# Softmax heads and stick-breaking heads in a pipeline of pairs, in a two-layer decoder trunk on one core

## The chip, the cores and the metric

The kernel runs on one core of a Trainium2 chip. The metric is the device time of one execution in microseconds. The median of three runs of the kernel before is 1323.23 us.

## The reference

Two layers, each with two gated feed-forward blocks around a mixer and a cross attention. The change touches the mixer alone:

```python
SEQ, D_MODEL, HEAD_DIM = 256, 1024, 64
N_FOX, N_DSA, N_SB = 6, 5, 5

def hybrid_mixer(h, positions, w_in, b_fgate, w_fox_out, w_dsa_out, w_sb_out, w_out):
    proj = h @ w_in
    ...
    # FOX: softmax(q k^T * scale + c_q - c_k, causal) v, c = cumsum of log forget gates
    o_fox = fox_attention(fq, fk, fv, log_f).reshape(b, s, FOX_W)
    # DSA: softmax over the top 64 keys of an index score
    o_dsa = dsa_sparse_attention(dq, dk, dv, q_idx, k_idx, w_idx, topk).reshape(b, s, DSA_W)
    # stick-breaking: a = exp(log_sigmoid(z) + sum of log_sigmoid(-z) over the keys between)
    o_sb = stick_breaking_attention(sq, sk, sv).reshape(b, s, SB_W)
    g = jax.nn.sigmoid(gates.reshape(b, s, N_BRANCH, D_MODEL))
    merged = g[:, :, 0] * (o_fox @ w_fox_out) + g[:, :, 1] * (o_dsa @ w_dsa_out) + g[:, :, 2] * (o_sb @ w_sb_out)
    return merged @ w_out
```

## The kernel before

Activations lie with features on the partitions (`xT`, eight tiles of 128 x 256). Every projection is three fp32r matmuls per 128 x 128 weight tile (`mm3`, L139 to L141): weight high by activation high, high by low, low by high. `load_w` brings a weight tile by DMA (SyncE's queue, `wraw`, three buffers), casts the high part on ScalarE (L92, `wh`, five buffers) and subtracts the low part on VectorE or sometimes GpSimd (L86, `wl`, five buffers). Matmuls of attention are plain fp32.

The mixer of a layer is written in this order: index heads and their top-k mask; FOX (three pairs of heads, L665 to L688); DSA (two pairs and a head, from L691); gate projections 0 to 4 (`gate_proj`) and the first sigmoids; stick-breaking (two pairs and a head, L780 to L815); `merge(0)`; the transposes of the memory (`transposed`, L243) with its squares and their statistics (`stats`, L197 and L199; `newton` with Ln and Exp makes the scale `rm` from them); gate projections 5 to 11; `sigmoids(4, 12)`; `merge(1)`; the keys of the cross attention from the memory; `merge(2)`; the split of the merged branches; `w_out`.

The code only gives dependencies. The order on each engine is made by a list scheduler that works through a simulated timeline, so projections of later parts are drawn in between attention steps. `tc.issue_after(x)` puts what follows behind x, if both are on the same engine. PSUM has three banks `acc` for projections, two `qk` for scores, two `tr` for transposes and statistics, one `ops` for products with v.

A softmax pair runs so: scores of two heads (L671 adds the key decay through a mask matmul, L675 is q times k with 64 rows for each head, on the two halves of the rows), logits into `w384` on VectorE, maximum, Exp on ScalarE, scaling by the reciprocal sum; `softmax_pv` then transposes (L606), copies to SBUF on ScalarE and multiplies with v (L618, L619). A stick-breaking pair has scores (L792), Abs, Exp and Ln on ScalarE, a split into high and low part, a running sum by matmuls with a triangular matrix `negu` into the `qk` banks (L804 to L808), two additions and an Exp, and the product with v.

`table(name)` loads a set of ScalarE's function tables. It stands behind all activations collected in `tabs["ops"]` since the last load, and each `tact` stands behind the load:

```python
def table(name):
    with ExitStack() as es:
        for i in tabs["ops"]:
            es.enter_context(tc.issue_after(i.ins))
        tabs["load"] = ACT.preload_act_table_set(name)
    tabs["ops"] = []
```

`sigmoids(c0, c1)` loads the table of the sigmoid, does the gates c0 to c1 and loads the table of Ln and Exp again. In `merge(br)` four accumulators `acc` are filled in turn, and VectorE multiplies each with its gate (L737), which frees the bank.

Of the kernel before, what the change touches and what calls it, by code (L numbers as in the profile page):

```python
# [9 lines left out]
F32 = mybir.dt.float32  # L10
# [3 lines left out]
OP = mybir.AluOpType  # L14
# [18 lines left out]
def trunk(ctx: ExitStack, tc: tile.TileContext, x, mem, positions, ffn1_norm, ffn1_w_gu, ffn1_w_down,  # L33
# [426 lines left out]
    def mixer_cross(l):  # L460
# [4 lines left out]
        with tc.tile_pool(name="mix", bufs=1) as mp:  # L465
# [122 lines left out]
            def softmax_pv(lgs, v, h0, ot):  # L588


                for p in lgs:
                    nm = mp.tile([128, 2], F32, name="nm", bufs=4)
                    sm = mp.tile([128, 2], F32, name="sm", bufs=4)
                    for t, (c0, c1) in enumerate((Q0, Q1)):
                        DVE.tensor_reduce(nm[:, t:t + 1], p[:, c0:c1], axis=AX.X, op=OP.max, negate=True)
                        tact(p[:, c0:c1], p[:, c0:c1], AF.Exp, bias=nm[:, t:t + 1], accum_out=sm[:, t:t + 1])
                    rs = mp.tile([128, 2], F32, name="rsm", bufs=4)
                    DVE.reciprocal(rs, sm)
                    for t, (c0, c1) in enumerate((Q0, Q1)):
                        last = DVE.tensor_scalar(p[:, c0:c1], p[:, c0:c1], rs[:, t:t + 1], None, op0=OP.mult)  # L600
                pTs = []
                for p in lgs:
# [4 lines left out]
                    pT = w384()  # L607
                    last_copy = ACT.activation(pT, ps[:, :384], AF.Copy)
                    pTs.append(pT)
                with tc.issue_after(last_copy.ins):  # L610
                    for i, pT in enumerate(pTs):
                        pv(ot, v, h0 + i, pT[:, 0:256], pT[:, 256:384])
# [53 lines left out]
            ofox = []  # L666
            for j in range(NFOX // 2):
# [9 lines left out]
                ot = o_ps()  # L677
                lgs = []
                for i, ps in enumerate(bank):
                    h = 2 * j + i  # L680
                    lg = w384()
                    DVE.scalar_tensor_tensor(lg[:, 0:128], ps[:, 0:128], cq[:, 0, h:h + 1], cmask[:, 0:128],
                                             op0=OP.add, op1=OP.add)
                    DVE.scalar_tensor_tensor(lg[:, 128:384], ps[:, 256:512], cq[:, 1, h:h + 1], cmask[:, 128:384],
                                             op0=OP.add, op1=OP.add)
                    lgs.append(lg)
                softmax_pv(lgs, fv, 2 * j, ot)
                ofox.append(hsplit(ot, 2))  # L688
# [11 lines left out]
            odsa = []  # L700
            for j in range(3):
                nh = 2 if j < 2 else 1
                bank = scores(dT[0][j], dT[1][j], nh)
                ot = o_ps()
                lgs = []
                for i, ps in enumerate(bank):
                    lg = w384()
                    DVE.tensor_tensor(lg, ps[:, :384], dmask, op=OP.add)
                    lgs.append(lg)
                softmax_pv(lgs, dv, 2 * j, ot)  # L710
                odsa.append(hsplit(ot, nh))
# [68 lines left out]
            for j in range(3):  # L780
                nh = 2 if j < 2 else 1

                zm = mp.tile([128, 2, 384], F32, name="zm", bufs=1)
                az = mp.tile([128, 2, 384], F32, name="az", bufs=1)
                sph = mp.tile([128, 2, 384], F32R, name="sph", bufs=1)
                spl = mp.tile([128, 2, 384], F32R, name="spl", bufs=1)
                zm, az, sph, spl = zm[:, :nh], az[:, :nh], sph[:, :nh], spl[:, :nh]
                bank = [qk_ps() for _ in range(nh)]
                for c, q0, k0 in ((0, 0, 0), (256, 128, 128)):
                    for i, ps in enumerate(bank):  # L790
                        b = slice(64 * i, 64 * i + 64)
                        PE.matmul(ps[:, c:c + 256 - q0], sk[j][b, k0:k0 + 128], sq[j][b, q0:], start=True, stop=True)  # L792
                for i, ps in enumerate(bank):
                    DVE.tensor_tensor(zm[:, i], ps[:, :384], smask, op=OP.add)
                ACT.activation(az, zm, AF.Abs)
                tact(az, az, AF.Exp, scale=-1.0)
                tact(az, az, AF.Ln, bias=1.0)
                DVE.scalar_tensor_tensor(az, zm, 0.0, az, op0=OP.max, op1=OP.add)
                split(sph, spl, az)
                ps0, ps1 = qk_ps(), qk_ps()  # L800
                p0 = ps0[:, :nh * 256].rearrange("p (h n) -> p h n", h=nh)
                p1 = ps1[:, :nh * 256].rearrange("p (h n) -> p h n", h=nh)
                for v in (sph, spl):
                    PE.matmul(p0, negu, v[:, :, 0:256], start=v is sph, stop=False)  # L804
# [154 lines left out]
```

## Time and profile before

| | us |
|---|---|
| median of three runs | 1323.23 (1323.03 to 1323.39) |
| profiled execution, whole time | 1323.02 |
| its span in the trace | 1321.3 |
| TensorE busy | 1305.2 |
| VectorE busy | 894.0 |
| ScalarE busy | 746.3 |
| GpSimd busy | 295.8 |

The profiled execution is one more run, within 0.2 us of the median; its span leaves out 1.7 us around the work. The mixer of layer 1 lies at about 198 to 445 us of the span, that of layer 2 at about 850 to 1093 us. In a timeline row the first number is the start, the second how long the group of equal instructions took. Matmuls overlap in the pipeline, so the pace is the distance of starts, not the length in the row.

### The profile page before, as it was taken

The page shows a single profiled execution, that of the slowest core. Times are in us where ns is not written, and L with a number is a line of the kernel's source. Part 1 is how long each engine was busy: PE and PEld are TensorE (multiplying, and loading weights), DVE is VectorE, ACT ScalarE, POOL GpSimd, SP SyncE. Part 2 cuts the span into 40 slices and gives each one's busy share as a digit, 9 for nine tenths or more (in the row PEclk, how much of TensorE's full clock was granted, in tenths as well). Part 3 has the DMA queues.
Part 4 walks back from the last instruction along what each step waited for, and adds up shares of the span by engine and source line. Part 5 has one row for each costly group of instructions (what it writes and reads, how often), then busy time and mean ns, then how long its engine had stood idle before and what let it go on. Part 6 is the DMA issues. An engine that isn't in the chain of part 4 may idle for free.

```text
span 1321.3 us, 26329 instructions
## 1 busy us (share of the span) xinstructions
PE 1305.2 (99%) x10746; PEld 1273.2 (96%) x10746; DVE 894.0 (68%) x1389; ACT 746.3 (56%) x1191; POOL 295.8 (22%) x267
## 2 busy tenths in 40 slices
PE   8999999999999999999999999999999999999997
PEld 7999998999999999999999999998999999999987
DVE  6866656966769776665666665569767686866644
ACT  6555544466775575554465554444667755655543
POOL 3211024322314121111121110243224230311100
PEclk9999999999999999999999999999999999999999
DMA  8555655544646555666655565645355655566551
GB/s 256 192 191 186 221 162 154 174 142 124 187 133 218 163 179 172 197 196 202 194 190 192 192 204 180 197 137 177 103 166 165 199 192 161 178 195 196 196 181 62
DMA packets 220712, 234.65 MB, mean 178 GB/s; under 512 B 8656, under 2 KB 209968, under 8 KB 220592
## 3 DMA queue, kind: packets, MB, share of 16 engines
q1 hardware_dynamic: 219904, 231.87, 55.1%
q8 instruction: 84, 1.38, 0.5%
q0 software_dynamic: 240, 0.55, 0.1%
q10 hardware_dynamic: 448, 0.57, 0.1%
q14 instruction: 36, 0.29, 0.1%
HBM read 231.91 MB, written 1.05 MB: 176 GB/s over the span
## 4 chain that ended last, share of the span: by engine, by line
PE 94%; DVE 2%; DMA 1%; issue 1%; POOL 1%; ACT 1%; DVEq 0%; ACTq 0%; POOLq 0%
PE acc L139 29%; PE acc L141 28%; PE acc L140 28%; DVE wl L86 1%; PE qk L553 1%; PE ops L618 1%; PE qk L675 1%; DMA wraw<-in_ffn_w_gu_dram 1%; DVE t L154 1%; PE ops L619 1%; PE tr L606 0%; POOL it L527 0%; DMA wraw<-in_w_in_dram 0%; PE qk L861 0%; PE qk L792 0%
## 5 line engine op out<-in xcount | busy, mean ns | idle before, releaser
L86 DVE TENSOR_TENSOR wl<-wraw,wh 128x1024 fp32r<-128x1024 f32 (+4 forms) x427 | 512.7, 1204 | 224.2 <-ACT wh L92 210.9
L92 ACT ACTIVATE wh<-wraw 128x1024 fp32r<-128x1024 f32 (+4 forms) x471 | 465.5, 994 | 245.1 <-PE acc L140 156.6
L141 PE MATMUL acc<-xh,wl 128*128 128x256 f32 x2032 | 563.5, 278 | 0.9 <-DVE wl L86 0.9
L139 PE MATMUL acc<-xh,wh 128*128 128x256 f32 x2032 | 563.9, 279 | 0.0
L140 PE MATMUL acc<-xl,wh 128*128 128x256 f32 x2032 | 563.7, 278 | 0.0
L139 PEld LDWEIGHTS acc<-xh,wh 128*128 128x128 f32 x2032 | 381.2, 188 | 3.8 <-issue 3.3
L141 PEld LDWEIGHTS acc<-xh,wl 128*128 128x128 f32 x2032 | 381.8, 188 | 2.4 <-DVE wl L86 1.7
L140 PEld LDWEIGHTS acc<-xl,wh 128*128 128x128 f32 x2032 | 382.2, 188 | 0.8 <-issue 0.7
L383 POOL TENSOR_TENSOR hm<-sg,gu 128x256 f32<-128x256 f32 x88 | 85.0, 966 | 385.2 <-ACT sg L69 385.2
L141 PE MATMUL acc<-hh,wl 128*128 128x256 f32 x528 | 145.3, 276 | 0.0
L140 PE MATMUL acc<-hl,wh 128*128 128x256 f32 x528 | 145.3, 276 | 0.0
L139 PE MATMUL acc<-hh,wh 128*128 128x256 f32 x528 | 144.3, 276 | 0.0
L86 POOL TENSOR_TENSOR wl<-wraw,wh 128x1024 fp32r<-128x1024 f32 (+4 forms) x44 | 89.9, 2043 | 211.9 <-ACT wh L92 174.1
L69 ACT ACTIVATE sg<-gu 128x256 f32<-128x256 f32 x88 | 36.7, 417 | 120.4 <-DVE gu L379 120.4
L141 PEld LDWEIGHTS acc<-hh,wl 128*128 128x128 f32 x528 | 99.1, 188 | 0.0
L140 PEld LDWEIGHTS acc<-hl,wh 128*128 128x128 f32 x528 | 99.1, 188 | 0.0
L139 PEld LDWEIGHTS acc<-hh,wh 128*128 128x128 f32 x528 | 98.5, 188 | 0.0
L379 DVE TENSOR_TENSOR gu<-acc,rs_r 128x512 f32<-128x512 f32 x88 | 60.3, 686 | 42.3 <-PE acc L141 42.2
L230 POOL TENSOR_TENSOR sqa<-sqa,sq 128x256 f32<-128x256 f32 x54 | 51.9, 960 | 138.8 <-ACT sq L225 137.2
L153 ACT ACTIVATE hh<-hm 128x256 fp32r<-128x256 f32 x88 | 36.1, 410 | 54.0 <-POOL hm L383 54.0
L154 DVE TENSOR_TENSOR hl<-hm,hh 128x256 fp32r<-128x256 f32 x88 | 37.0, 421 | 42.5 <-ACT hh L153 42.4
L141 PE MATMUL acc<-wh,xl 128*128 128x320 f32 (+1 forms) x192 | 61.0, 318 | 0.0
(283 smaller groups left out, 1971.3 us busy)
## 6 DMA issues: line engine op xcount, KB each, us to landing
wraw<-in_ffn_w_gu_dram SPq DMA_DIRECT2D x87, 1024.0 KB, 5.3
wraw<-in_w_in_dram SPq DMA_DIRECT2D x34, 1024.0 KB, 5.4
wraw<-in_ffn_w_down_dram SPq DMA_DIRECT2D x28, 896.0 KB, 4.9
wraw<-in_ffn_w_down_dram SPq DMA_DIRECT2D x18, 1024.0 KB, 5.2
wraw<-in_w_in_dram SPq DMA_DIRECT2D x20, 640.0 KB, 4.1
wraw<-in_ca_w_kv_dram SPq DMA_DIRECT2D x8, 1024.0 KB, 5.0
wraw<-in_w_out_dram SPq DMA_DIRECT2D x8, 1024.0 KB, 5.0
wraw<-in_ca_w_q_dram SPq DMA_DIRECT2D x4, 1024.0 KB, 5.3
```

The costliest lines, as they stand in the source:

```text
L69: i = ACT.activation(*a, **k)
L86: share["last"] = eng.tensor_tensor(lo, raw, h.bitcast(F32), op=OP.subtract)
L92: ACT.activation(h, raw, AF.Copy)
L139: PE.matmul(ps, a[0], b[0], start=first, stop=False)
L140: PE.matmul(ps, a[0], b[1], start=False, stop=False)
L141: PE.matmul(ps, a[1], b[0], start=False, stop=last)
L153: ACT.activation(h, src, AF.Copy)
L154: DVE.tensor_tensor(lo, src, h.bitcast(F32), op=OP.subtract)
L230: POOL.tensor_tensor(n, sqacc[0], sq, op=OP.add)
L379: DVE.tensor_tensor(gu, ps.rearrange("p (i n) -> p i n", i=2), rb2(r), op=OP.mult)
L383: POOL.tensor_tensor(hm, sg, gu[:, 1], op=OP.mult)
L553: PE.matmul(ps[:, c:c + n], q[b, qs], k[b, 0:n], start=True, stop=True)
```

## The change

Softmax heads: `softmax_pv`, which did one pair to its end, is replaced by `attention(npairs, v, score, logits)`, which runs over `npairs + 2` steps. In step n TensorE has one stretch: the transposes of pair n-1, the product with v of pair n-2, the scores of pair n. The stretch stands behind the last scaling of pair n-1 by means of `issue_after` on its first transpose. Then come the copies of the transposes, the logits and the softmax of pair n. FOX and DSA hand over their own functions for scores and logits.

Stick-breaking heads: the loop over three pairs becomes five steps of the same kind. A step holds the running sum of pair n-1, the product with v of pair n-2 and the scores of pair n. The running sum goes into the two `tr` banks, no longer `qk`, with the low part first; the last Exp is one for each head and goes into `w384`.

```diff
-            def softmax_pv(lgs, v, h0, ot):
...
-                pTs = []
-                for p in lgs:
-                    ps = tr_ps()
-                    with tc.issue_after(last.ins):
-                        for j in range(3):
-                            PE.transpose(ps[:, j * 128:(j + 1) * 128], p[:, j * 128:(j + 1) * 128], ident)
...
+            def attention(npairs, v, score, logits):
+                prs, pTs, out, last = {}, {}, [], None
+                for n in range(npairs + 2):
+                    bank, tps, ot = [], [], None
+                    with ExitStack() as es:
+                        if last is not None:
+                            es.enter_context(tc.issue_after(last.ins))
+                        for p in prs.pop(n - 1, ())[::-1]:
+                            ps = tr_ps()
+                            for j in (2, 1, 0):
+                                i = PE.transpose(ps[:, j * 128:(j + 1) * 128], p[:, j * 128:(j + 1) * 128], ident)
+                                if not tps and j == 2:
+                                    es.enter_context(tc.issue_after(i.ins))
+                            tps.insert(0, ps)
+                        if n - 2 in pTs:
+                            ot = o_ps()
+                            for i, pT in enumerate(pTs[n - 2]):
+                                pv(ot, v, 2 * n - 4 + i, pT[:, 0:256], pT[:, 256:384])
+                        if n < npairs:
+                            bank = score(n)
+                    if tps:
+                        pTs[n - 1] = []
+                        for ps in tps:
+                            pT = w384()
+                            last = ACT.activation(pT, ps[:, :384], AF.Copy)
+                            pTs[n - 1].append(pT)
+                    lgs = [logits(n, i, ps) for i, ps in enumerate(bank)]
+                    if ot is not None:
+                        out.append(hsplit(ot, len(pTs.pop(n - 2))))
...
+                            last = DVE.tensor_scalar(p[:, c0:c1], p[:, c0:c1], rs[:, t:t + 1], None, op0=OP.mult)
+                    prs[n] = lgs
+                return out
...
-            for j in range(3):
...
-                ps0, ps1 = qk_ps(), qk_ps()
...
+            for n in range(3 + 2):
...
+                    if 0 <= n - 1 < 3:
...
+                        ps0, ps1 = tr_ps(), tr_ps()
...
+                        for v in (spl, sph):
+                            i = PE.matmul(p0, negu, v[:, :, 0:256], start=v is spl, stop=False)
+                            if v is spl:
+                                es.enter_context(tc.issue_after(i.ins))
...
+                    if 0 <= n - 2:
+                        ot = o_ps()
+                        for i, p in enumerate(prs[n - 2]):
+                            pv(ot, sv, 2 * n - 4 + i, p[:, 0:256], p[:, 256:384])
+                    if n < 3:
+                        bank = [qk_ps() for _ in range(nh)]
...
+                    prs[n - 1] = [w384() for _ in range(mh)]
+                    for i, p in enumerate(prs[n - 1]):
+                        tact(p, mz[:, i], AF.Exp)
+                    last = tabs["ops"][-1]
```

What the scheduler makes of it, at three places of layer 1. Line numbers of the later parts of the mixer are larger by 12 or more in the changed kernel (L671 and L675 are L689 and L693, L606 is L601, L737 is L749).

TensorE at the scores of FOX pair 2. `qk_3169` and `qk_3170` are the banks of its two heads, `acc` rows are projections. Before:

```order
L140 MATMUL acc_3498<-wl_3484,xh2_84 128x320
L671 MATMUL qk_3169<-cneg_80,sel_79 128x256 x2
L675 MATMUL qk_3169<-t1_3009,t1_2885 128x128
L675 MATMUL qk_3169<-t1_3009,t1_2885 128x256
L141 MATMUL acc_3498<-wh_3483,xl2_92 128x320
L671 MATMUL qk_3170<-cneg_80,sel_79 128x256 x2
L675 MATMUL qk_3170<-t1_3009,t1_2885 128x128
L675 MATMUL qk_3170<-t1_3009,t1_2885 128x256
L139 MATMUL acc_3497<-wh_3483,xh3_85 128x320
```

After:

```order
L139 MATMUL acc_3699<-xh5_87,wh_3695 128x256
L601 MATMUL tr_3146<-ident_73,w384_3123 128x128 x3
L601 MATMUL tr_3150<-ident_73,w384_3120 128x128 x3
L689 MATMUL qk_3154<-cneg_80,sel_79 128x256 x2
L689 MATMUL qk_3155<-cneg_80,sel_79 128x256 x2
L693 MATMUL qk_3154<-t1_3009,t1_2885 128x128
L693 MATMUL qk_3155<-t1_3009,t1_2885 128x128
L693 MATMUL qk_3154<-t1_3009,t1_2885 128x256
L693 MATMUL qk_3155<-t1_3009,t1_2885 128x256
L140 MATMUL acc_3699<-xl5_95,wh_3695 128x256
```

The two heads' scores were apart with a projection between; now they are one piece, behind the six transposes of pair 1.

TensorE at the statistics of the memory (L197). `acc_4749` and `acc_4810` are gate projections; `acc_5013`, `acc_5032`, `acc_5064`, `acc_5083` are the four accumulators of merge(1). Before:

```order
L141 MATMUL acc_4749<-xh7_89,wl_4746 128x256
L197 MATMUL tr_4542<-sqa_4540,triones_74 128x256 [waits Pool_49]
L199 MATMUL tr_4542<-triones_74,sqa_4540 128x1 x2
L139 MATMUL acc_4810<-xh0_82,wh_4802 128x256
L140 MATMUL acc_4810<-xl0_90,wh_4802 128x256
```

After:

```order
L145 MATMUL acc_5032<-osp_3683,wl_5009 128x256
L146 MATMUL acc_5032<-osp_3684,wl_5009 128x256
L197 MATMUL tr_4549<-sqa_4547,triones_74 128x256 [waits Pool_49]
L199 MATMUL tr_4549<-triones_74,sqa_4547 128x1 x2
L139 MATMUL acc_5064<-osp_3647,wh_5055 128x256 [waits DVE_49,Activation_49]
...
L146 MATMUL acc_5064<-osp_3684,wl_5060 128x256
L139 MATMUL acc_5083<-osp_3647,wh_5055 128x256 [waits DVE_49,PE_49]
```

The statistics moved from between two gate projections to behind the second accumulator of merge(1). `acc_5083` begins with a wait for VectorE.

ScalarE at Ln and Exp of these statistics (`rs_a`, `rs_b`) and the sigmoids of gates 4 to 11 (`t2`). Before:

```order
L69 ACTIVATE rs_a_4547<-rs_m_4546 128x258 [waits DVE_49]
L153 ACTIVATE sph_4320<-az_4319 128x384 [waits DVE_49]
L69 ACTIVATE rs_b_4548<-rs_a_4547 128x258 [waits Activation_49]
L92 ACTIVATE wh_4928<-wraw_4922 128x1024 [waits PE_49]
L92 ACTIVATE wh_4997<-wraw_4993 128x1024 [waits DMAHW2_49,PE_49,Pool_49]
L69 ACTIVATE az_4319<-zm_4318 128x384 [waits DVE_49,Activation_49]
L64 ACT_TABLE_LOAD
L69 ACTIVATE t2_3992<-t2_3992 128x512
L69 ACTIVATE t2_4615<-t2_4615 128x512
```

After:

```order
L92 ACTIVATE wh_5167<-wraw_5163 128x1024 [waits DMAHW1_49,PE_49]
L92 ACTIVATE wh_5171<-wraw_5163 64x512 [waits DMAHW3_49,PE_49]
L69 ACTIVATE rs_a_4554<-rs_m_4553 128x258 [waits DVE_49]
L69 ACTIVATE rs_b_4555<-rs_a_4554 128x258 [waits Activation_49]
L64 ACT_TABLE_LOAD
L69 ACTIVATE t2_3992<-t2_3992 128x512
L69 ACTIVATE t2_4622<-t2_4622 128x512
...
L64 ACT_TABLE_LOAD
L92 ACTIVATE wh_5218<-wraw_5214 128x1024 [waits DMAHW4_49,PE_49]
```

The table load now follows `rs_b` directly, and `rs_a` ahead of it waits for `rs_m` on VectorE. Six more sigmoids are left out before the last load shown. VectorE around `rs_m` and the product with gate 4, `acc_5006` before and `acc_5013` after. Before:

```order
L86 TENSOR_TENSOR wl_5049<-wraw_5044,wh_5048 128x1024 [waits DMAHW5_49,Activation_49]
L86 TENSOR_TENSOR wl_5053<-wraw_5044,wh_5052 64x512 [waits PE_49,DMAHW7_49,Activation_49,Pool_49]
L719 TENSOR_TENSOR t2_4981<-acc_4932,rs_r_2511 128x512 [waits PE_49]
L86 TENSOR_TENSOR wl_5098<-wraw_5095,wh_5097 128x1024 [waits DMAHW0_49,DVE_49,Activation_49]
L737 TENSOR_TENSOR t2_3992<-acc_5006,t2_3992 128x512 [waits PE_49]
L86 TENSOR_TENSOR wl_5102<-wraw_5095,wh_5101 128x1024 [waits PE_49,Activation_49]
```

After:

```order
L86 TENSOR_TENSOR wl_5109<-wraw_5102,wh_5108 128x1024 [waits PE_49,Activation_49]
L86 TENSOR_TENSOR wl_5168<-wraw_5163,wh_5167 128x1024 [waits DVE_49,DMAHW1_49,PE_49,Activation_49]
L187 TENSOR_SCALAR rs_m_4553<-tr_4549 128x258 [waits PE_49]
L190 TENSOR_TENSOR rs_a_4554<-rs_b_4555 128x258 [waits Activation_49]
L191 SCALAR_TENSOR_TENSOR rs_a_4554<-rs_a_4554,rs_m_4553 128x258 [waits DVE_49]
L192 SCALAR_TENSOR_TENSOR rs_r_4556<-rs_a_4554,rs_b_4555 128x258 [waits DVE_49]
L749 TENSOR_TENSOR t2_3992<-acc_5013,t2_3992 128x512 [waits Activation_49]
```

Two weight splits (`wl_5109`, `wl_5168`, both with a wait for TensorE), `rs_m` and the rest of the statistics now stand ahead of the product with gate 4, and that product waits for ScalarE.

## Rows read from the trace of the kernel before

**Rows 1.** The page: busy time of the engines, granted clock, chain that ended last.

```profile
PE 1305.2 (99%) x10746; PEld 1273.2 (96%) x10746; DVE 894.0 (68%) x1389; ACT 746.3 (56%) x1191; POOL 295.8 (22%) x267
...
PEclk9999999999999999999999999999999999999999
...
PE 94%; DVE 2%; DMA 1%; issue 1%; POOL 1%; ACT 1%; DVEq 0%; ACTq 0%; POOLq 0%
```

**Rows 2.** Waits of TensorE: for what, total us, times, longest.

```profile
PE tr L270 <- DMA xin<-in_x_dram: 5.0, 1, 5.0
```

**Rows 3.** Busy time by window, FOX of layer 2: length, PE, PEld, DVE, ACT, POOL.

```profile
905.00:915.00 10.00, 10.00 (x65) 9.07 (x64) 9.59 (x29) 5.90 (x13) 3.09 (x4) 1.00 0.46 142
```

**Rows 4.** TensorE's timeline, FOX pairs 1 and 2 of layer 1: start, us, instruction.

```profile
256.14 0.64 PE L671 MATMUL qk<-cneg,sel 128*128 128x256 f32 x4
256.70 0.93 PE L675 MATMUL qk<-t,t 64*128 64x128 f32 x8
257.56 0.42 PE L139 MATMUL acc<-wh,xh 128*128 128x320 f32 x1
257.81 0.31 PE L140 MATMUL acc<-wl,xh 128*128 128x320 f32 x1
257.96 0.31 PE L141 MATMUL acc<-wh,xl 128*128 128x320 f32 x1
...
261.04 0.40 PE L671 MATMUL qk<-cneg,sel 128*128 128x256 f32 x2
...
262.47 0.39 PE L671 MATMUL qk<-cneg,sel 128*128 128x256 f32 x2
...
263.90 0.31 PE L140 MATMUL acc<-wl,xh 128*128 128x320 f32 x1
```

**Rows 5.** TensorE's timeline, memory statistics of layer 1 and projections behind.

```profile
373.66 0.59 PE L197 MATMUL tr<-sqa,triones 128*128 128x256 f32 x2
...
374.66 0.28 PE L140 MATMUL acc<-xl,wh 128*128 128x256 f32 x1
...
376.94 0.28 PE L139 MATMUL acc<-xh,wh 128*128 128x256 f32 x1
```

**Rows 6.** TensorE's timeline, FOX pair 3 of layers 1 and 2.

```profile
272.43 0.48 PE L671 MATMUL qk<-cneg,sel 128*128 128x256 f32 x2
...
274.76 0.28 PE L140 MATMUL acc<-xl,wh 128*128 128x256 f32 x1
...
921.38 0.47 PE L671 MATMUL qk<-cneg,sel 128*128 128x256 f32 x2 [0.27 <-DVE w L684]
...
924.37 0.28 PE L139 MATMUL acc<-xh,wh 128*128 128x256 f32 x1
```

**Rows 7.** DMA issues of the memory tiles: count, KB each, median us to landing.

```profile
mi<-in_mem_dram SPq DMA_DIRECT2D x8, 256.0 KB, 5.2
```

**Rows 8.** ScalarE's timeline, statistics and sigmoids of layer 1.

```profile
376.63 0.42 ACT L69 ACTIVATE rs_a<-rs_m 128x258 f32<-128x258 f32 x1 [0.60 <-DVE rs_m L187]
...
383.83 1.28 ACT L64 ACT_TABLE_LOAD   x1
385.13 3.24 ACT L69 ACTIVATE t<-t 128x512 f32<-128x512 f32 x6
```

**Rows 9.** VectorE's timeline, statistics and merge(1) of layer 1.

```profile
376.18 0.43 DVE L187 TENSOR_SCALAR rs_m<-tr 128x258 f32<-128x258 f32 x1
...
394.78 0.68 DVE L737 TENSOR_TENSOR t<-acc,t 128x512 f32<-128x512 f32 x1
395.99 1.93 DVE L86 TENSOR_TENSOR wl<-wraw,wh 128x1024 fp32r<-128x1024 f32 x1 [0.53 <-PE acc L141]
...
398.45 1.21 DVE L86 TENSOR_TENSOR wl<-wraw,wh 128x1024 fp32r<-128x1024 f32 x1
```

**Rows 10.** TensorE's timeline, the first projections of the program.

```profile
9.54 0.41 PE L140 MATMUL acc<-xl,wh 128*128 128x256 f32 x1
9.75 0.41 PE L141 MATMUL acc<-xh,wl 128*128 128x256 f32 x1
```

More of the change, by code (lines that the diff above doesn't have):

```diff
@@ new lines, in attention @@
+            def attention(npairs, v, score, logits):
[27 more added lines that the diff above has]
+                        out.append(hsplit(ot, len(pTs.pop(n - 2))))
+                    for p in lgs:
+                        nm = mp.tile([128, 2], F32, name="nm", bufs=4)
+                        sm = mp.tile([128, 2], F32, name="sm", bufs=4)
+                        for t, (c0, c1) in enumerate((Q0, Q1)):
+                            DVE.tensor_reduce(nm[:, t:t + 1], p[:, c0:c1], axis=AX.X, op=OP.max, negate=True)
+                            tact(p[:, c0:c1], p[:, c0:c1], AF.Exp, bias=nm[:, t:t + 1], accum_out=sm[:, t:t + 1])
+                        rs = mp.tile([128, 2], F32, name="rsm", bufs=4)
+                        DVE.reciprocal(rs, sm)
+                        for t, (c0, c1) in enumerate((Q0, Q1)):
+                            last = DVE.tensor_scalar(p[:, c0:c1], p[:, c0:c1], rs[:, t:t + 1], None, op0=OP.mult)
+                    prs[n] = lgs
+                return out
@@ L664, in mixer_cross, with fox_score @@
             DVE.tensor_tensor(cneg[32:32 + NFOX], ps[:NFOX, :256], cneg[:NFOX].bitcast(F32), op=OP.subtract)
-            ofox = []
-            for j in range(NFOX // 2):
+            def fox_score(j):
                 bank = [qk_ps() for _ in range(2)]
@@ L676, in mixer_cross, with fox_logits @@
                                   start=False, stop=c == 256)
[L677 to L688, printed above, removed]
+                return bank
+            def fox_logits(j, i, ps):
+                h = 2 * j + i
+                lg = w384()
+                DVE.scalar_tensor_tensor(lg[:, 0:128], ps[:, 0:128], cq[:, 0, h:h + 1], cmask[:, 0:128],
+                                         op0=OP.add, op1=OP.add)
+                DVE.scalar_tensor_tensor(lg[:, 128:384], ps[:, 256:512], cq[:, 1, h:h + 1], cmask[:, 128:384],
+                                         op0=OP.add, op1=OP.add)
+                return lg
+            ofox = attention(NFOX // 2, fv, fox_score, fox_logits)
             dT = []
@@ L699, in mixer_cross, with dsa_logits @@
             dv = tok_v(proj_tok(DSA0 + 640, 320), 320)
-            odsa = []
-            for j in range(3):
[L702 to L711, printed above, removed]
+            def dsa_logits(j, i, ps):
+                lg = w384()
+                DVE.tensor_tensor(lg, ps[:, :384], dmask, op=OP.add)
+                return lg
+            odsa = attention(3, dv, lambda j: scores(dT[0][j], dT[1][j], 2 if j < 2 else 1), dsa_logits)
             gates = []
@@ L779, in mixer_cross @@
             osb = []
[L780 to L789, printed above, removed]
-                    for i, ps in enumerate(bank):
[L791 to L799, printed above, removed]
-                ps0, ps1 = qk_ps(), qk_ps()
[L801 to L804, printed above, removed]
-                for v in (sph, spl):
-                    PE.matmul(p0[:, :, 128:256], negones, v[:, :, 256:384], start=False, stop=v is spl)
-                for v in (sph, spl):
-                    PE.matmul(p1[:, :, 0:128], negu, v[:, :, 256:384], start=v is sph, stop=v is spl)
-                DVE.tensor_tensor(zm[:, :, 0:256], p0, zm[:, :, 0:256], op=OP.add)
-                DVE.tensor_tensor(zm[:, :, 256:384], p1[:, :, 0:128], zm[:, :, 256:384], op=OP.add)
-                tact(az, zm, AF.Exp)
-                ot = o_ps()
-                for i in range(nh):
-                    pv(ot, sv, 2 * j + i, az[:, i, 0:256], az[:, i, 256:384])
-                osb.append(hsplit(ot, nh))
```

53 lines of the change are left out of this document (37 added, 16 removed).

## Prediction

> **What bounds the kernel now.** I read the page's busy table and chain first [rows 1]: TensorE works 1305.2 us of a span of 1321.3, and 94% of the chain that ended last is TensorE's. The waits of TensorE say what the other 16 us are: 5.0 us for the input at the start [rows 2], the rest in small pieces, none of them in the merges. So the end moves by what TensorE's queue gets shorter, and by every new wait on that queue; what the other engines gain or lose is worth nothing until TensorE waits for it. VectorE is the engine to fear: in the stretch of the FOX heads of layer 2 it is busy 9.59 of 10 us [rows 3].
>
> **What the change takes away.** A stretch of score matmuls has a price that hardly depends on what it holds. One FOX pair in one piece [rows 4]: from 256.14 to the second projection after it at 257.81 are 1.67 us; less four mask matmuls at the fp32r pace of 0.114 us (20 steps from 374.66 to 376.94 [rows 5]) and one projection of 0.15 (257.81 to 257.96), 1.06 us stay for eight score records (256.70). The next pair is cut in two by a projection: 261.04 to 262.47 is 1.43 us, less two mask matmuls and one projection is 1.05 us, for one head with four records, and the other head, 262.47 to 263.90, costs the same again. The two heads lie on the two halves of the rows, and one head alone takes as long as both. The Trainium skill says why ("TensorE: Matmul & The Clock Gate", Part 3): small matmuls on different row groups run beside each other, so a lone one saves nothing. The trace agrees: 1.05 us for one head, 1.06 for two.
>
> Before, four of the six FOX pairs over the two layers are cut: pairs 2 and 3 of each layer. The order shows each pair of after in one piece, so each gives back its second half [rows 6]. Pair 2, twice: 1.05 each, 2.1 us. Pair 3 of layer 1, behind its predecessor's product with v: 272.43 to 274.76 is 2.33 us, less four mask matmuls and a projection 1.76, so 0.7 us. Pair 3 of layer 2: 921.38 to 924.37 is 2.99, less four mask matmuls and three projections 2.19, so 1.1 us, and the wait of 0.27 us ahead of it goes too. Together 4.2 us. DSA pairs, stick-breaking pairs and index heads have uncut scores to begin with, or are untouched.
>
> The order has 104 attention stretches of fp32 before and 63 after. Where different kinds of work merge into one stretch (transposes, product with v, scores), what can go is the slow return to projections: 257.56 to 257.81 is 0.25 us where the pace is 0.15, so 0.1 us each. Some 25 merges of that kind give 0 to 2.5 us. Pair 3 of layer 1 speaks for the low end: its scores already ran straight behind a product with v, and cost no less than a half and a whole in the sum above. I take 0.5 us, with the transposes of one pair that no longer are cut. **Gain on TensorE: 4.7 us**, bounds 4.2 and 6.7.
>
> **What it costs inside the steps.** Each step's stretch now starts behind its latest input: the transposes of pair n and the scores of pair n+1 wait for the last scaling of pair n. The work that covers this is 65 to 85 projections between two steps, 7 to 10 us, against a softmax on a VectorE that in layer 2's FOX has 0.4 of 10 us to spare [rows 3]. Softmax work itself is the same; stick-breaking has one more exponential per pair, on ScalarE, which has room (56% [rows 1]). I found no step in which the cover clearly fails; the thinnest is FOX pair 1 in layer 2. The products with negu now sit in the two `tr` banks that the memory transposes (L243) also use, so these come later: the loads of the third and fourth memory tile go out behind the first transposes, with a median of 5.2 us to land [rows 7], and TensorE has 42 matmuls, 4.8 us, and a product with v until it needs the third. That is just covered, too. For all of this I put 0.5 us, bounds 0 and 2.
>
> **What it costs in merge(1): the main term.** Because L243 comes later, so do the statistics of the memory (L197). Before, they ran at 373.66 [rows 5], far ahead of merge(1); now the order puts them in the middle of merge(1), behind the second of its four accumulators. Behind them hangs a chain. The table of the sigmoids may only be loaded behind the Ln and Exp of these statistics (`tabs["ops"]`), and the eight sigmoids of gates 4 to 11 stand behind the table on ScalarE. Merge(1)'s first product with gate 4 (L749 on VectorE) needs the first sigmoid, and the fourth accumulator reuses the bank of the first (three `acc` banks), so TensorE stands until L749 is done. In the before trace sigmoids began at 385.13 and the product at 394.78 [rows 8, 9]: 9.7 us of room.
>
> Count from the start of L197, called A. On VectorE two weight splits stand ahead of rs_m, and both wait for matmuls at the very end of the second accumulator, so they begin at A: 2 times 1.21 us [rows 9]. Then rs_m with its hand-over, 376.18 to 376.63, 0.45. On ScalarE rs_a 0.42 and rs_b, the same form, 0.43 with hand-over. The table 1.30 (383.83 to 385.13) [rows 8]. The first sigmoid 0.54 (3.24 for six), 0.6 with the hand-over. L749 0.68 (as L737 at 394.78). Sum 2.42 + 0.45 + 0.85 + 1.30 + 0.6 + 0.7 = 6.3 us. TensorE has meanwhile: L197 and L199 0.9 (373.66 to 374.66 holds one projection) and the third accumulator, 16 projections at 0.114, 1.8: 2.7 us. **A new wait of 3.6 us, and layer 2 has the same order: 7.2 us.** The bounds: 2.4 us a layer if one split is not ahead; 5.0 if both splits take 1.93 us, as one did at 395.99 [rows 9]. Behind the wait nothing else is late: the weight casts (L92) that queue on ScalarE behind the eight sigmoids and a second table are needed 80 matmuls later, some 9 us. The wait at the split of the merged branches stays: its chain is unchanged.
>
> A page disagrees on one link. The Trainium skill ("ScalarE: Activation LUTs", What ACT_TABLE_LOAD costs) adds a drain of about 1.38 us to the 1.28 us of a load. The trace shows the 1.28 and no drain: the sigmoid starts 0.02 us behind. By the page the estimate would be 1.4 us longer per layer, 1329.0 in all.
>
> **The sum.** Profiled execution 1323.02, 0.2 below the median of 1323.23: -4.7 + 0.5 + 7.2 = +3.0, so 1326.2 against the median. With all bounds on one side this case reaches from 1321 to 1331; the gain near its low end and one bound at a time make 1323.5 to 1329.5.
>
> **Rivals.**
> - *The wait in merge(1) is hidden.* If the bank is not the one I read, or the sigmoids get ahead of it, the 4.7 us stand alone: 1323.2 - 4.7 + 0.5 = 1319.0, down to 1318. For it: the profile before has no wait in merge(1). Against it: every link is an instruction in the order of after, and two of three engines are held by TensorE itself, so being early elsewhere does not help.
> - *Half of it.* The chain in one layer only, or shortened to 2 us in both: 1323.2 - 4.2 + 4 = 1323. For it: the splits ahead of rs_m hang on slots whose release I read from the order alone.
> - *The clock falls in the wait.* At the start TensorE waits 5.0 us [rows 2], and then its fp32r matmuls start 0.21 us apart (9.54 to 9.75) where they need 0.114 [rows 10]: half pace, which is what 1.2 instead of 2.4 GHz would give, though the granted clock reads 9 in the first slice as in all others [rows 1]. From the first matmul at about 5.0 to 9.75 at half pace loses some 2.4 us. If a wait of 3.6 us does the same, each layer pays up to that: 1328 to 1332, I say 1330. Against it: these waits are shorter than that of the start. The Trainium skill ("TensorE: Matmul & The Clock Gate", What's actually happening) has a clock gate that halves the clock after idling and gives it back after sustained work; by that rule this rival is possible, and no other wait of the before trace is long enough to try it.
>
> **How the numbers follow.** The wait as computed: 0.62. Hidden: 0.18. Half: 0.10. Clock: 0.10. A measurement of this kernel tells a change of about 0.2%, 2.6 us, from none: 1320.6 and 1325.9 are the bounds. The main case lies astride the upper one, a little more than half above: slower 0.34, same 0.28. Hidden is nearly all faster, half is same, clock is slower. Faster 0.18, same 0.38, slower 0.44. The range takes in the hidden case and most of the main one: 1318.3 to 1329.
>
> **What would show it.** Right: FOX scores in eight records without a projection between; a new row among TensorE's waits, acc for VectorE's product at L749, two times, some 3.6 us each; ScalarE with rs_a, rs_b, table and sigmoids in one run inside merge(1). Wrong: no such wait (then 1319), or a wait of L243 for the memory loads, or of the transposes (L601) for VectorE, of over 1 us, or projections 0.21 us apart behind the wait.

## The result and the profile after

The changed kernel takes 1335.03 us, median of four runs (1333.65 to 1336.94), beside 1323.13 for the kernel before on the same chips: ratio 1.0092, with a 95% interval of 1.0080 to 1.0105. It is slower by 11.9 us, and outside the predicted range of 1318.3 to 1329. The profiled execution is the fastest of the four; its span of 1331.9 us is 10.6 over that of before.

Busy time, granted clock and chain of the changed kernel, as [rows 1] of before:

```profile
PE 1305.2 (98%) x10746; PEld 1273.7 (96%) x10746; DVE 903.5 (68%) x1389; ACT 748.6 (56%) x1195; POOL 294.5 (22%) x267
...
PEclk9999999999999999999999999999999999999999
...
PE 89%; DVE 6%; issue 2%; DMA 1%; ACT 1%; POOL 1%; SPq 0%; DVEq 0%; ACTq 0%; POOLq 0%
```

TensorE is busy for the same 1305.2 us, in a longer span. The gain on its work is there, but it is hidden in this line, since slower matmuls count as busy. The chain shows the loss: VectorE went from 2 to 6%. Waits of TensorE by what it waited for (total, times, longest):

```profile
PE acc L139 <- DVE t L749: 7.1, 2, 3.6
...
PE tr L601 <- DVE w L629: 3.5, 3, 2.8
...
PE tr L807 <- DVE spl L846: 1.1, 1, 1.1
```

Three lines are new: 7.1 us in two waits for L749, the product with gate 4 in merge(1); 3.5 us in three for the scaling L629 ahead of the transposes; 1.1 us for the low part ahead of the running sum. By the distance of the starts around them, which takes in the emptying and filling of the pipeline, they come to 7.5, 4.1 and 1.3 us. The wait in merge(1), layer 1, runs on three engines. First TensorE (start, us, instruction):

```profile
392.97 0.59 PE L197 MATMUL tr<-sqa,triones 128*128 128x256 f32 x2
...
395.58 0.28 PE L146 MATMUL acc<-osp,wl 128*128 128x256 f32 x1
399.42 0.55 PE L139 MATMUL acc<-osp,wh 128*128 128x256 f32 x1 [3.57 <-DVE t L749]
...
400.63 0.41 PE L141 MATMUL acc<-osp,wl 128*128 128x256 f32 x1
400.84 0.41 PE L145 MATMUL acc<-osp,wl 128*128 128x256 f32 x1
...
402.85 0.28 PE L139 MATMUL acc<-t,wh 128*128 128x256 f32 x1
```

The statistics at 392.97 are where the order had put them. The third accumulator ends at 395.58, and the fourth begins at 399.42, 3.57 us late. Then the starts lie 0.21 us apart (400.63 to 400.84), not the 0.114 of [rows 5], until about 402.6. VectorE and ScalarE in the same time:

```profile
393.01 2.36 DVE L86 TENSOR_TENSOR wl<-wraw,wh 128x1024 fp32r<-128x1024 f32 x2 [1.13 <-PE acc L141]
395.29 0.42 DVE L187 TENSOR_SCALAR rs_m<-tr 128x258 f32<-128x258 f32 x1
...
398.59 1.89 DVE L749 TENSOR_TENSOR t<-acc,t 128x512 f32<-128x512 f32 x3 [0.59 <-ACT t L69]
```

```profile
395.74 0.42 ACT L69 ACTIVATE rs_a<-rs_m 128x258 f32<-128x258 f32 x1 [2.28 <-DVE rs_m L187]
396.19 0.42 ACT L69 ACTIVATE rs_b<-rs_a 128x258 f32<-128x258 f32 x1
396.63 1.28 ACT L64 ACT_TABLE_LOAD   x1
397.92 4.27 ACT L69 ACTIVATE t<-t 128x512 f32<-128x512 f32 x8
```

This is the chain of the prediction link by link: two splits, rs_m, rs_a, rs_b, table, first sigmoid, L749. From the start of L197 it took 392.97 to 399.42, 6.45 us; 6.3 had been computed. The granted clock by windows (the value behind POOL is the granted clock):

```profile
400.00:405.00 5.00, 5.00 (x34) 5.00 (x34) 2.44 (x4) 4.97 (x8) 3.65 (x4) 0.73 0.00 0
405.00:410.00 5.00, 5.00 (x46) 5.00 (x46) 3.92 (x4) 3.24 (x5) 0.76 (x1) 1.00 0.67 222
...
1055.00:1060.00 5.00, 5.00 (x34) 5.00 (x33) 2.71 (x4) 4.95 (x8) 3.65 (x4) 0.70 0.02 5
```

0.73 of full in the 5 us behind the wait: 1.2 GHz for part of it, then 2.4 again. Layer 2 repeats it (1055 to 1060, 0.70). That cost is in no line of waits: the 16 matmuls from 399.42 to 402.85 take 3.43 us, where the pace gives 1.82, so 1.6 us a layer.

The longest wait of a step, in FOX of layer 2, on TensorE, VectorE and GpSimd:

```profile
929.67 0.28 PE L140 MATMUL acc<-xl,wh 128*128 128x256 f32 x1
932.73 0.85 PE L601 MATMUL tr<-ident,w 128*128 128x128 f32 x6 [2.79 <-DVE w L629]
```

```profile
926.24 0.76 DVE L629 TENSOR_SCALAR w<-w,rsm 128x128 f32<-128x128 f32 x2
...
929.96 2.63 DVE L629 TENSOR_SCALAR w<-w,rsm 128x128 f32<-128x128 f32 x2
```

```profile
929.86 2.38 POOL L86 TENSOR_TENSOR wl<-wraw,wh 128x1024 fp32r<-128x1024 f32 x1 [3.21 <-ACT wh L92]
```

The last two scalings take 2.63 us where the two ahead of them took 0.76. They begin 0.1 us behind a weight split on GpSimd that takes 2.38, and the first of them, 2.37 us long, ends 0.1 us behind it.

The wait of 1.1 us in stick-breaking of layer 2 has such a neighbour too. Ahead of the low part stands a cast on VectorE (L492), which takes 0.29 us at its shortest, and here 2.38, up to the end of a split on GpSimd:

```profile
993.81 2.38 DVE L492 CAST osp<-cneg 64x256 fp32r<-64x256 f32 x1
```

```profile
993.08 2.96 POOL L86 TENSOR_TENSOR wl<-wraw,wh 128x1024 fp32r<-128x1024 f32 x1 [7.13 <-PE acc L141]
```

The balance: new waits 7.5 + 4.1 + 1.3 = 12.9 and half pace 3.2 are 16.1 us. In this execution TensorE was 0.8 us further on at the end of the first 32 us than in that of before. The span grew by 10.6, so 16.1 - 0.8 - 10.6 = 4.7 us are what the work on TensorE, with the wait of 0.3 us in FOX [rows 6] that is gone, got shorter by. This is a remainder, from one execution of each kernel.

### The profile page after: what moved, and what is told of

Read it like the earlier page. It is cut to its first block, busy times and chain, and to the rows that moved or that the text cites. A ratio compares the mean times of both kernels' runs of the same rounds, so it can differ in the third digit from the quotient of the medians.

```text
span 1331.9 us, 26326 instructions
## 1 busy us (share of the span) xinstructions
PE 1305.2 (98%) x10746; PEld 1273.7 (96%) x10746; DVE 903.5 (68%) x1389; ACT 748.6 (56%) x1195; POOL 294.5 (22%) x267
## 4 chain that ended last, share of the span: by engine, by line
PE 89%; DVE 6%; issue 2%; DMA 1%; ACT 1%; POOL 1%; SPq 0%; DVEq 0%; ACTq 0%; POOLq 0%
PE acc L140 27%; PE acc L139 27%; PE acc L141 27%; DVE wl L86 2%; PE qk L553 1%; DMA wraw<-in_ffn_w_gu_dram 1%; PE ops L637 1%; DVE t L154 1%; PE tr L601 0%; PE ops L638 0%; DVE sc L583 0%; POOL it L527 0%; DMA wraw<-in_w_in_dram 0%; PE qk L894 0%; DVE m L582 0%
```

## Experiments

Every run is compared with runs of the kernel before on the same chip, whose median lay between 1322.8 and 1323.5. "After" is the changed kernel.

### Is it the table behind the statistics?

sig_first is after with the statistics written behind the sigmoids:

```diff
-            rm = stats(sqacc[0])
 
             gate_proj(5, 12)
             sigmoids(4, 12)
+            rm = stats(sqacc[0])
```

> The changed kernel with one line moved: the statistics of the memory are written behind sigmoids(4, 12), so the table of the sigmoids no longer stands behind their Ln and Exp. Everything else, the transposes in the tr banks too, is as in the changed kernel (1335.0 us). Theory (the wait in merge(1) comes through the table): the two waits for L749 (7.1 us) go, and with them the half pace behind them (3.2 us): 1324.7 us. Rival (the bank is freed late because VectorE has two weight splits ahead, whatever the table does): a wait of over 1 us per layer stays, 1328 or more.

1326.60 us, ratio 1.0021 (1.0012 to 1.0031): 8.4 us less than after. The waits of 3.6 us are gone; a shorter one for L749 has come later, behind the statistics in their new place:

```profile
PE tr L601 <- DVE w L629: 3.5, 3, 2.8
PE acc L139 <- DVE t L749: 2.0, 2, 1.0
```

2.0 us in two waits instead of 7.1 account for the distance to 1324.7. The link through the table is shown: only the order of two statements changed.

mem_qk is after with the transposes of the memory in the `qk` banks, so that the statistics run ahead of merge(1):

```diff
-                ps = transposed([mi[:, t] for t in range(2)], 0)
+                ps = transposed([mi[:, t] for t in range(2)], 0, qk_ps)
```

> The changed kernel with the transposes of the memory (L243) in the qk banks instead of tr. The order puts the statistics about 100 matmuls earlier, ahead of merge(1). Theory (late statistics are what starts the chain): no wait for L749, no half pace, 1324.7 us, up to 1 us more if the memory transposes now wait for stick-breaking scores. Rival (VectorE is late in merge(1) by itself): the waits stay, 1335 us.

1326.39 us, ratio 1.0021 (1.0011 to 1.0030). No wait for L749; the wait for the split of the merged branches grew from 1.1 to 2.5 us. Both ways out agree within their spread: late statistics start the chain, and the table carries it.

### Does standing still cost the clock?

fill puts 30 useless matmuls into the wait of merge(1):

```diff
...
+                        if br == 1 and c == 3:
+                            d = o_ps()
+                            with tc.issue_after(mark1[0].ins):
+                                for _ in range(30):
+                                    mark1[0] = PE.matmul(d[:, :256], negu, xh[0], start=True, stop=True)
                         ps = acc_ps()
...
```

> The changed kernel with 30 matmuls of no use (fp32r, 256 columns, some 3.4 us) between the third and the fourth accumulator of merge(1), where TensorE waited 3.6 us; the wait itself is untouched. Theory (the half pace of some 3 us behind the wait comes from TensorE having stood still): the projections behind keep 0.114 us and the granted clock stays at 1.00, 1335.0 - 3.2 = 1331.8 us. Rival (the half pace has to do with what runs there, not with the standing still): 1335 us.

1333.34 us, ratio 1.0075 (1.0060 to 1.0090). TensorE at the same place, and the granted clock:

```profile
396.71 3.66 PE L746 MATMUL ops<-xh,negu 128*128 128x256 f32 x30
400.45 0.36 PE L139 MATMUL acc<-osp,wh 128*128 128x256 f32 x1
```

```profile
400.00:405.00 5.00, 4.92 (x44) 4.75 (x43) 3.33 (x5) 4.97 (x9) 4.62 (x4) 1.00 0.01 3
...
930.00:935.00 5.00, 2.30 (x10) 2.16 (x11) 4.28 (x4) 1.50 (x3) 2.21 (x1) 0.78 0.86 286
```

The fourth accumulator begins as late as in after, 3.7 us behind the third, and the granted clock from 400 to 405 is 1.00. So the half pace in merge(1) came with the standing still, and goes when TensorE is kept at work. The median fell by 1.7 us, less than the 3.2 expected. Here the traces can settle it, since TensorE has the same order in both but for the useless matmuls: from one matmul to its twin, fill gains 1.5 us in merge(1) of layer 1 and 1.6 in that of layer 2, together about the 3.2 that were expected. It loses 1.6 us in FOX of layer 2, where in this execution the wait of 2.8 us also had half pace behind it (0.78 in the second row), which the profiled execution of after did not, and it came 1.1 us later out of the first 32 us.

softmax_only has the FOX and DSA steps of after and the stick-breaking loop of before (no new code).

> The changed kernel with the stick-breaking loop of the kernel before: only FOX and DSA are in steps. Theory (the gain on TensorE is 4.7 us, the waits of the steps, 4.1 us in FOX, eat it up, and the wait in merge(1) belongs to stick-breaking in the tr banks): no wait for L749, 1323.1 - 4.7 + 4.1 = 1322.5 us. Rival (the waits of the steps also come from the stick-breaking part): 1318.5 us.

1326.21 us, ratio 1.0021 (1.0012 to 1.0030), over both expectations. No wait for L749. The steps' waits are all still there (L601 3.5 us), a wait of 1.6 us for the low part in stick-breaking has come, and behind the wait in FOX of layer 2 the transposes run slow:

```profile
928.73 1.51 PE L601 MATMUL tr<-ident,w 128*128 128x128 f32 x6 [2.79 <-DVE w L629]
```

```profile
925.00:930.00 5.00, 2.21 (x15) 2.04 (x14) 5.00 (x5) 1.67 (x2) 2.37 (x1) 0.81 0.75 234
930.00:935.00 5.00, 5.00 (x35) 4.30 (x34) 2.07 (x6) 1.63 (x4) 0.00 (x0) 0.85 0.54 185
```

Six transposes took 1.51 us here, 0.85 in after. The same wait of 2.8 us was followed by half pace in this trace, in fill's, in sig_first's and in mem_qk's (0.66 from 930 to 935 in both), and by full pace in after's. That fits the wide spread of all kernels with this wait (1324.74 to 1327.38 here; 1322.96 to 1324.21 for before), and so does the mean granted clock on record for every run: the two fastest runs of softmax_only (1324.74 and 1324.81) had 0.999, the eight others (1326.07 and more) 0.997 or 0.998, and those of before 0.998 or 0.999.

sb_only is the other half: stick-breaking in steps, softmax heads as before.

> The kernel before with the stick-breaking steps of the change alone, softmax heads as before. Theory (the wait in merge(1) and the half pace behind it belong to the stick-breaking part, whatever the softmax heads do): two waits for L749 of 3.6 us, half pace behind each, 1323.5 + 7.1 + 3.2 = 1333.8 us. Rival (it needs both parts, because the softmax steps push the stick-breaking later): under 1328 us.

1333.70 us, ratio 1.0080 (1.0066 to 1.0093), as the theory said, with the same wait:

```profile
PE acc L139 <- DVE t L737: 7.1, 2, 3.6
```

One part of the theory does not hold in the trace. Half pace follows the wait of layer 1, and full pace the wait of layer 2, which is just as long (3.57 us from 1050.9 to 1054.45):

```profile
400.00:405.00 5.00, 3.98 (x22) 4.01 (x23) 2.53 (x4) 4.98 (x9) 3.76 (x3) 0.66 0.05 16
...
1055.00:1060.00 5.00, 5.00 (x46) 5.00 (x45) 2.69 (x4) 4.97 (x8) 4.89 (x4) 1.00 0.01 3
```

This execution (1332.18) is the fastest of the four; the slowest two, 1334.40 and 1334.50, had a mean granted clock of 0.995 and 0.996 where it had 0.997. What decides whether the clock falls is open.

So the stick-breaking part alone loses 10.7 us and the softmax steps alone 2.7, together somewhat more than the whole change.

### What holds the scaling?

scale_act is softmax_only with the scaling on ScalarE:

```diff
-                            last = DVE.tensor_scalar(p[:, c0:c1], p[:, c0:c1], rs[:, t:t + 1], None, op0=OP.mult)
+                            last = ACT.activation(p[:, c0:c1], p[:, c0:c1], AF.Copy, scale=rs[:, t:t + 1])
```

> Steps for FOX and DSA, stick-breaking as before (1326.2 us), and the scaling by the reciprocal sum on ScalarE instead of VectorE. In the traces the last scaling ahead of the longest wait of the transposes took 2.4 us instead of 0.3, over the same time as a weight split on GpSimd. Theory (the wait of 2.8 us in layer 2 is VectorE's scaling held by GpSimd's split): the wait of the transposes falls from 3.5 to under 1 us, and with it the slow stretch behind: 1322.0 us. Rival (the step waits because the whole softmax is late): a wait of over 2 us stays, 1325 or more.

1320.50 us, ratio 0.9980 (0.9971 to 0.9990): 5.7 us less than softmax_only (5.4 by the ratios, since the chips differ), and faster than before.

```profile
PE tr L601 <- ACT w L629: 0.7, 1, 0.7
```

so_no_gpsimd is softmax_only with `share["pool"] = 0` in place of 3 at the head of the mixer: all weight splits on VectorE.

> Steps for FOX and DSA, stick-breaking as before (1326.2 us), and no weight split on GpSimd in the mixer: all on VectorE. Theory (the scaling is held by GpSimd's split): no scaling takes over 0.4 us; but VectorE has up to 22 splits of 1.2 us more per layer, and where it has nothing to spare the steps wait for that: 1322 to 1326 us. Rival (GpSimd has nothing to do with the long scaling): scalings of over 2 us stay.

1320.31 us, ratio 0.9980 (0.9971 to 0.9989). The longest of the 44 scalings (nanoseconds, min/median/max), first in before, then in after, then here:

```profile
L600 DVE TENSOR_SCALAR w<-w,rsm x44: 261/314/350, 264.9 to 965.5; 128x128 f32<-128x128 f32 x22, 128x256 f32<-128x256 f32 x22
```

```profile
L629 DVE TENSOR_SCALAR w<-w,rsm x44: 273/342/2368, 264.2 to 976.3; 128x128 f32<-128x128 f32 x22, 128x256 f32<-128x256 f32 x22
```

```profile
L629 DVE TENSOR_SCALAR w<-w,rsm x44: 266/343/979, 265.5 to 976.7; 128x128 f32<-128x128 f32 x22, 128x256 f32<-128x256 f32 x22
```

2.37 us, the length of a GpSimd split, has become 0.98 (beside other work of GpSimd, an operation of 1.02 us on the DSA mask), and no wait at L601 is left. VectorE took on 22 splits a layer, and one wait for it grew: that for the split of the merged branches, from 1.1 to 2.2 us. Moving the scaling away and moving the splits away give the same time, but not by the same sum. Without splits in the mixer TensorE also loses its waits for GpSimd in the index heads (L538, 2.3 us in softmax_only), which scale_act keeps, and its busy time is 2.4 us more than in scale_act (1303.9 beside 1301.5); why, was not looked for. So the equal times alone do not show one cause. both, with the two together, is the better test.

> Steps for FOX and DSA, stick-breaking as before, no weight split on GpSimd in the mixer, and the scaling on ScalarE. If the two ways out are one cause, the second adds nothing to the first: 1320.4 us. If they are two, each with its own wait: 1318 us.

1320.65 us, ratio 0.9983 (0.9974 to 0.9992). With the splits gone, moving the scaling as well adds nothing: it was the splits that made the scaling slow.

### Do the two causes add up?

no_gpsimd is after with `share["pool"] = 0`.

> The whole change with no weight split on GpSimd in the mixer, and nothing else altered: one of the two causes taken out of the changed kernel (1335.0 us). Theory (the two add up): no scaling of over 1 us, no wait of over 1 us at L601, the two waits for L749 and the half pace behind them stay: 1335.0 - 5.5 = 1329.5 us. Rival (VectorE with all splits makes the chain in merge(1) longer): 1332 or more.

1343.02 us, ratio 1.0150 (1.0137 to 1.0164): 8 us worse than after, not 5.5 better. The waits at L601 are gone, as expected. But with other work on VectorE the scheduler made another order, and put the last memory transposes and the statistics straight ahead of the fourth accumulator:

```profile
PE tr L197 <- POOL sqa L230: 8.5, 2, 4.2
PE acc L139 <- DVE t L749: 8.4, 2, 4.2
```

```profile
395.00:400.00 5.00, 1.87 (x6) 1.60 (x6) 0.91 (x2) 1.11 (x4) 1.93 (x3) 0.59 0.30 100
400.00:405.00 5.00, 1.67 (x8) 1.70 (x9) 3.17 (x6) 4.94 (x10) 1.73 (x2) 0.50 0.00 0
405.00:410.00 5.00, 5.00 (x27) 5.00 (x27) 3.07 (x3) 4.59 (x7) 3.31 (x3) 0.55 0.00 0
```

Now TensorE waits for the sum of squares and then for the whole chain, 8.4 us a layer, and has half its clock for most of 15 us. The term that a cause is worth can't be taken from one order to another where the change lets the order move.

sums_no_gpsimd takes out both causes: after with the running sums in the `qk` banks and no split on GpSimd.

```diff
-                        ps0, ps1 = tr_ps(), tr_ps()
+                        ps0, ps1 = qk_ps(), qk_ps()
```

> The whole change with both causes taken out: the running sums of the stick-breaking steps in the qk banks as before the change (so the statistics of the memory run ahead of merge(1) again), and no weight split on GpSimd in the mixer. Theory (the change loses by the late statistics and by scalings held by GpSimd, and by nothing else): no wait for L749, none of over 1 us for the transposes, 1320.0 us, as with the softmax steps alone. Rival (the stick-breaking steps cost something of their own): 1322 us or more.

1319.80 us, ratio 0.9977 (0.9968 to 0.9986): faster than before, as expected. No wait for L749 or L601 is left.

```profile
PE acc L140 <- DVE t L154: 1.9, 2, 1.0
PE acc L141 <- DVE wl L86: 0.8, 1, 0.8
```

### What is the gain worth?

scores_whole is before with one part alone: both heads' scores of a FOX pair in one piece.

```diff
+                for i, ps in enumerate(bank):
+                    m = PE.matmul(ps[:, 0:256], sel[:, 2 * j + i], cneg, start=True, stop=False)
+                with tc.issue_after(m.ins):
+                    for i, ps in enumerate(bank):
+                        PE.matmul(ps[:, 256:512], sel[:, 2 * j + i], cneg, start=False, stop=False)
...
```

> The kernel before, with one part of the change alone: of a FOX pair the scores of both heads are pinned behind the mask matmul that comes free last, so that each pair is one piece of eight score records, as in the changed kernel. No steps, no merging of transposes and products with v. Theory (the gain of the change is the four second halves of cut pairs, 4.2 us, and what the change adds to it is waiting): 1323.5 - 4.2 = 1319.3 us, with the scores in uncut pieces of 1.06 us. Rival (a pair in one piece makes the logits of its first head later, and VectorE, with 0.4 of 10 us to spare, gives the time back as a wait of the transposes): 1322 to 1324 us.

1321.14 us, ratio 0.9986 (0.9977 to 0.9995): 1.8 us, under half of the 4.2. FOX pair 2 of layer 2 in one piece:

```profile
906.08 0.28 PE L670 MATMUL qk<-cneg,sel 128*128 128x256 f32 x1
...
907.23 0.28 PE L670 MATMUL qk<-cneg,sel 128*128 128x256 f32 x1
907.34 0.40 PE L673 MATMUL qk<-cneg,sel 128*128 128x256 f32 x2
907.67 0.93 PE L677 MATMUL qk<-t,t 64*128 64x128 f32 x8
```

The scores are whole, but three small waits have come (0.5 us at L606, 0.5 at L618, 0.4 at the mask matmul), and TensorE's busy time fell by 2.9 us (1302.3). How the rest went was not tested; in the trace some products with v now come in two pieces.

pool_late is softmax_only with GpSimd off the splits up to the end of DSA, and on again behind it (`share["pool"] = 0` at the head of the mixer, 3 behind `odsa`).

> Steps for FOX and DSA, stick-breaking as before, GpSimd without weight splits up to the end of DSA and with every third one behind it, as before the change. Without GpSimd in the whole mixer the wait for the split of the merged branches had grown from 1.1 to 2.2 us. Theory (GpSimd only harms beside the scalings and helps VectorE elsewhere): 1.0 us under the run without GpSimd, 1319.3 us. Rival (it makes no difference where the splits lie): 1320.3 us.

1318.55 us (1318.43 to 1318.76), ratio 0.9968 (0.9956 to 0.9981): the lowest median of all, 4.2 us under the kernel before; its interval and that of so_no_gpsimd overlap. The wait for the merged branches is back at 1.1 us. GpSimd has not left the attention altogether: splits of weights that are used later still run there, and two scalings still take over 2 us beside them. TensorE waits at L601 no more:

```profile
L629 DVE TENSOR_SCALAR w<-w,rsm x44: 271/340/2495, 265.5 to 971.4; 128x128 f32<-128x128 f32 x22, 128x256 f32<-128x256 f32 x22
```

So here a held scaling costs nothing as long as TensorE has other work.

before_pool_late has that line in the kernel before, without any of the change.

> The kernel before with one line of other kernels here: no weight split on GpSimd up to the end of DSA. No part of the change. With steps for FOX and DSA the same line gave 1318.55 us. If the gain of the change on TensorE is the 4.7 us of the prediction and GpSimd gives nothing by itself, 1322.8 us here. If GpSimd's absence also shortens the kernel before (its index heads wait 2.1 us for GpSimd), 1320.7 us, and the steps are worth only the rest, about 2.2 us.

1322.08 us, ratio 0.9991 (0.9982 to 1.0000). In between: about 1.2 of pool_late's 4.2 us are GpSimd's (0 to 2.4 by the interval), and the softmax steps are worth 3.0. The 1.2 fit the trace: TensorE's waits for GpSimd in the index heads (L538, 2.1 us in before) are gone, and its busy time is 0.8 us more. Its busy time in the two (before_pool_late, then pool_late) gives the 3.0 again, without a difference in waits:

```profile
PE 1306.0 (99%) x10746; PEld 1273.0 (96%) x10746; DVE 902.8 (68%) x1409; ACT 746.7 (57%) x1191; POOL 263.7 (20%) x247
```

```profile
PE 1302.9 (99%) x10746; PEld 1271.0 (97%) x10746; DVE 903.8 (69%) x1409; ACT 746.2 (57%) x1191; POOL 265.2 (20%) x247
```

sums_pool_late is the whole change with the sums in the `qk` banks and that line.

> The whole change with the running sums back in the qk banks and no weight split on GpSimd up to the end of DSA: both causes out, in the better way of the two. If the stick-breaking steps are worth nothing, 1318.6 us as with the softmax steps alone; if their merged stretches count, 0.5 us less for each layer, 1317.6 us; if they cost, over 1319.5 us.

1319.76 us, ratio 0.9973 (0.9962 to 0.9983), no faster than pool_late (0.9968). It has a wait of 1.1 us for the low part ahead of the running sum that pool_late does not have: VectorE's subtraction for it (L847) takes 2.90 us there, beside a GpSimd split of 2.39, where it took 0.94 in layer 1. The stick-breaking steps gain nothing that could be measured, here or in sums_no_gpsimd (0.9977 beside 0.9980 of so_no_gpsimd), where no such wait is left.

## Why the prediction was wrong, point by point

- **The gain of 4.7 us on TensorE** is right in kind, and its size stays open. The balance of after leaves 4.7, as a remainder of one execution; against a base with the same splits on GpSimd taken out (before_pool_late), the softmax steps are worth 3.0 to 3.1, under the lower bound of 4.2, and the stick-breaking steps nothing. One head's scores cost as much as two, as read from [rows 4]. That the gain can be had by pinning the scores alone, the prediction didn't say, and scores_whole shows less than half of it.
- **The wait in merge(1)** was right: 3.6 us a layer computed, 3.57 measured, 7.1 in all, by the chain named. sig_first, mem_qk and sb_only bear it out. The drain that the Trainium skill ("ScalarE: Activation LUTs", What ACT_TABLE_LOAD costs) adds to a table load doesn't show here either: load at 396.63 for 1.28 us, sigmoid at 397.92.
- **The waits inside the steps** were the step that failed: a term put at 0.5 us, bounds 0 and 2; measured 5.4 (4.1 at L601, 1.3 at L807). A wait at L601 of over 1 us was one of the prediction's own signs of being wrong. The prediction asked how much VectorE has to do, and found it nearly full [rows 3]. It did not ask what else can hold the last scaling, on which the step now hangs. In before that scaling never met a split on GpSimd (its longest is 0.35 us). In after eight of the 44 take 0.5 to 2.37 us, each beside work of GpSimd, and the cast ahead of L807 does the same. The Trainium skill ("SBUF — State Buffer", Who interferes with whom) says that a `tensor_scalar` in a two-port mode and a GpSimd instruction lock each other out for a whole instruction. The trace agrees: 2.37 us of scaling beside a split of 2.38. In which mode the scaling ran, no trace here shows.
- **The clock** was the second step that failed: it had no term in the sum. It was a rival with a chance of 0.10; in the profiled execution it happened in merge(1) of both layers, 1.6 us each, where 2.4 had been the price. The row of the start [rows 10] had shown it; "shorter than the wait of the start" was taken for a reason against, without a row for a wait of that length. The rule of the Trainium skill ("TensorE: Matmul & The Clock Gate", What's actually happening), that the clock halves after idling, agrees with these two waits (0.73 and 0.70 behind them) and with fill (1.00); sb_only's second wait of 3.57 us has 1.00 behind it, so such a wait need not bring the half pace.
- **The sign** was right, the size was not: 3.0 us forecast, 11.9 measured. In the profiled execution 4.9 us of step waits, 3.2 of half pace and 0.3 in merge(1) came on top, less 0.8 us that it was ahead at the start. The other 1.4 us are the distance of the median from that execution. The mean granted clocks of the four runs, from the fastest to the slowest 0.996, 0.996, 0.994 and 0.993, fit more half pace in the slower two; where it lay no trace shows.

## What to carry to other kernels

When a change moves work to other banks, look for what else is queued for those banks, and follow that to the last engine: here two PSUM banks moved statistics, and through a table load they stopped TensorE for 3.6 us. An estimate of a TensorE wait of some us needs a second term for the clock behind it, with a chance: here the same wait had half pace behind it in one trace and full pace in another. A step that hangs on one VectorE instruction needs that instruction free of GpSimd: taking off GpSimd the weight splits that the code has ahead of the end of DSA turned the softmax half of this change from 2.7 us slower into 4.2 faster than before (1.2 of it GpSimd's own).

## What the hardware showed that was not expected

- One VectorE scaling (`tensor_scalar`, fp32) took 2.37 us where the median is 0.34, beside a GpSimd split of 2.38 us; with no splits on GpSimd the longest was 0.98. A cast took 2.38 us beside a split of 2.96, and 0.29 at its shortest.
- TensorE's granted clock fell to 1.2 GHz after standing still for 3.6 us in three waits of four (after: both layers, 0.73 and 0.70; sb_only: layer 1, 0.66, and not layer 2, 1.00), and after 2.8 us in the traces of softmax_only, fill, sig_first and mem_qk, and not in that of after. Filled with useless matmuls, the same 3.7 us left it at 2.4 GHz. With two waits of 4.2 us close together (no_gpsimd) it was low in most of 15 us (0.59, 0.50 and 0.55 in three stretches of 5 us).
